# The q, k and v projections of a hybrid attention layer as one Strassen level

## The chip, the core and the metric

The kernel runs on one core of a Trainium2 chip. The metric is the device time of one execution in microseconds, the median of three runs. The profile shows one execution in which a hardware profiler recorded every instruction. The engines are TensorE (PE in the profile, PEld for its weight loads), VectorE (DVE), ScalarE (ACT), GpSimd (POOL) and SyncE (SP), which here issues nearly all transfers. Each engine takes its own instructions in the order in which the program lists them.

## The reference

One layer over 1024 tokens of width 1024, all in fp32:

```python
xn = rms_norm(x, norm_g)
proj = xn @ w_in                                  # [1024,1024] x [1024,4096]
qa, ka, va, za, qb, kb, vb, zb = split(proj)      # 512 columns each
qa, ka, qb, kb = rms_norm of each over groups of 64 columns
oa = diff_attention(qa, ka, va)                   # dense, two softmaxes a head
ya = rms_norm(oa) * silu(za)
yb = neighbourhood_attention(qb, kb, vb) * silu(zb)
x  = x + concat(ya, yb) @ w_out
x  = x + sigmoid(x @ w_ple_gate) * (p @ w_ple_proj)
```

The change concerns the six blocks kb, vb, qb, ka, va and qa of proj. The two gate blocks za and zb are computed later, beside the attention.

## The kernel before

Every large product is made of three matmuls: the operands are split into a high part in a reduced fp32 format and a low part that holds what is left, and high x high, high x low and low x high are added up in PSUM. A matmul takes 128 rows of depth, 128 tokens and 512 columns ("128x512").

The program first computes p @ w_ple_proj (lines with pps) and normalises x tile by tile. A tile is 128 tokens: `x_norm` (L228) gives xhat, `x_trans` (L240) or `x_trans_all` (L252) transposes it on TensorE, and ScalarE and VectorE take the high and the low part out of PSUM (xh, xl). Then the six blocks follow in the order kb, vb, qb, ka, va, qa, each over eight token tiles. `inproj` (L268) issues 8 x 3 matmuls for one block and tile, at L273, L274 and L275. The weights of a block come in four chunks: `load_w` (L147) loads 256 x 512 values (512 KB), 24 times in all; `split_w` (L152) multiplies them by the norm gain ng while it splits them, on ScalarE (L160) and VectorE (L161).

The result of two tiles stands in one PSUM buffer (ips). For a query or key block `qk_norm1` (L283) squares and sums it and takes the power -1/2 on GpSimd (L291, a 128x16 operand), `qk_norm2` (L294) scales it into qn, `qk_trans` (L299) transposes it (eight transposes, qtp), splits it, and the parts are stored in DRAM. For a value block `v_evac` (L344) copies or splits and stores it. The scaling and the transposes of two tiles come one and two tiles later in the order. Those of the last two tiles of qa stand inside the loop of neighbourhood attention (its rounds 1, 2 and 3, stores in round 4).

The order of every engine is that of the code, written out by hand. Transfers stand in SP's queue in that order too. While ScalarE, VectorE and GpSimd work on one tile, TensorE goes on with the next block's matmuls. GpSimd's part in the projection is the low part of half of the p weights (L172), the powers of the norms (L236 for x, L291), and the issue of a few casting transfers for the attention's constants. Neighbourhood attention begins with its scores (nsp, L534), VectorE's maximum and ScalarE's exponential (nas, L549 and L554), scaling (L562) and transposes (ntp, L572); dense attention follows, with the output projection and the gate behind it.

## Time and profile before

| | |
|---|---|
| median of three runs | 839.13 us (838.38 to 840.76) |
| the profiled execution: its span | 836.4 us |
| TensorE busy | 810.0 us, 97% |
| VectorE, ScalarE, GpSimd busy | 429.2, 395.6, 221.5 us |
| the matmuls of the six blocks | L273 to L275, 1152 of them |

The page gives no other time for the profiled execution than its span; the median of the timed runs lies 2.7 us above it. A busy time is the union of an engine's instructions; the mean duration of one matmul counts the overlap with its neighbour, so the pace of matmuls is read from starts. "Idle before, releaser" names what ended a wait.

### The profile page before, as it was taken

How to read it: one execution, taken by the hardware profiler on the slowest of the kernel's cores; microseconds unless marked ns; L12 is line 12 of the kernel's file. 1: busy time of each engine (PE TensorE's matmuls, PEld its weight loads, DVE VectorE, ACT ScalarE, POOL GpSimd, SP SyncE). 2: the span in 40 equal slices, each digit the busy share in tenths (PEclk: the TensorE clock that was granted, in tenths of full speed). 3: DMA queues.
4: the chain of work that ended last, by engine and by line, in shares of the span. 5: the costliest groups of instructions: out<-in, count | busy, mean ns of one | idle time of the engine just before them, and what ended most of it. 6: DMA issues, size and time to landing. Idle time of an engine off the chain costs nothing.

```text
span 836.4 us, 12140 instructions
## 1 busy us (share of the span) xinstructions
PE 810.0 (97%) x4386; PEld 673.8 (81%) x4386; DVE 429.2 (51%) x934; ACT 395.6 (47%) x776; POOL 221.5 (26%) x239
## 2 busy tenths in 40 slices
PE   8999999999999999699998999999999999999997
PEld 7788888888888887577876777888888878888885
DVE  4546521454432245356664678777777752732332
ACT  6435321233221214365655578889888861411120
POOL 1013100332211221011111124676767761200000
PEclk9999999999999999989999999999999999999999
DMA  8635333355353976657676778768685536323222
GB/s 295 217 126 199 111 122 124 76 128 148 113 191 131 251 177 193 177 144 194 161 201 198 180 238 217 210 149 222 171 236 157 160 107 247 124 76 101 86 91 88
DMA packets 110683, 136.72 MB, mean 163 GB/s; under 512 B 22904, under 2 KB 73752, under 8 KB 110624
## 3 DMA queue, kind: packets, MB, share of 16 engines
q1 hardware_dynamic: 108832, 130.19, 54.4%
q0 software_dynamic: 1792, 5.77, 2.3%
q8 instruction: 35, 0.57, 0.3%
q14 instruction: 24, 0.20, 0.1%
HBM read 93.95 MB, written 41.98 MB: 163 GB/s over the span
## 4 chain that ended last, share of the span: by engine, by line
PE 83%; DMA 6%; ACT 3%; DVE 3%; SPq 3%; issue 1%; POOL 1%; DVEq 0%; ACTq 0%; POOLq 0%
PE ips L273 10%; PE ips L275 10%; PE ips L274 10%; PE dsp L865 7%; PE gps L1060 3%; PE gps L1058 3%; PE gps L1059 3%; PE dtp L907 3%; PE ntp L572 2%; PE zps L469 2%; PE zps L471 2%; PE zps L470 2%; SPq L93 2%; PE pps L205 2%; PE npv L587 2%; PE dpv L934 2%
## 5 line engine op out<-in xcount | busy, mean ns | idle before, releaser
L273 PE MATMUL ips<-wh,xh 128*128 128x512 f32 x384 | 151.7, 395 | 0.0
L275 PE MATMUL ips<-wh,xl 128*128 128x512 f32 x384 | 149.8, 390 | 0.0
L274 PE MATMUL ips<-wl,xh 128*128 128x512 f32 x384 | 149.6, 389 | 0.0
L291 POOL TENSOR_TENSOR qrs<-qms,nhalf 128x16 f32<-128x16 f32 x16 | 50.3, 3143 | 186.0 <-DVE qms L289 175.0
L890 POOL TENSOR_TENSOR s<-s,s 128x1024 f32<-128x1024 f32 x32 | 77.2, 2412 | 58.1 <-ACT s L889 43.6
L275 PEld LDWEIGHTS ips<-wh,xl 128*128 128x128 f32 x384 | 72.1, 188 | 15.2
L273 PEld LDWEIGHTS ips<-wh,xh 128*128 128x128 f32 x384 | 72.1, 188 | 14.6 <-issue 0.3
L274 PEld LDWEIGHTS ips<-wl,xh 128*128 128x128 f32 x384 | 72.2, 188 | 14.3
L875 DVE CUSTOM_DVE_ANT_0 s<-dsp,T 128x1024 f32<-128x1024 f32 x64 | 77.7, 1215 | 0.0
L877 ACT ACTIVATE s<-s,dm 128x1024 f32<-128x1024 f32 x64 | 73.3, 1145 | 3.6 <-DVE dm L875 3.6
L865 PE MATMUL dsp<-K,Q 128*128 128x512 f32 x256 | 69.4, 393 | 1.4 <-DVE dm L875 1.4
L914 DVE TENSOR_TENSOR aTl<-dtp,aTh 128x512 fp32r<-128x512 f32 x64 | 44.2, 691 | 48.6 <-ACT aTh L908 48.6
L469 PE MATMUL zps<-xh,zw 128*128 128x512 f32 x128 | 54.7, 427 | 0.0
L865 PEld LDWEIGHTS dsp<-K,Q 128*128 128x128 f32 x256 | 46.1, 189 | 10.5 <-issue 1.3
L603 POOL TENSOR_TENSOR yb<-nay,yb 128x128 fp32r<-128x128 f32 x32 | 15.8, 493 | 146.1 <-ACT yb L602 146.1
L574 ACT ACTIVATE PT<-ntp 96x768 f32<-96x768 f32 (+1 forms) x32 | 25.9, 811 | 56.0 <-PE ntp L572 56.0
L471 PE MATMUL zps<-xh,zw 128*128 128x512 f32 x128 | 51.4, 402 | 0.0
L470 PE MATMUL zps<-xl,zw 128*128 128x512 f32 x128 | 51.3, 400 | 0.0
L1058 PE MATMUL gps<-wgh,x1h 128*128 128x512 f32 x128 | 50.4, 394 | 0.0
L1060 PE MATMUL gps<-wgh,x1l 128*128 128x512 f32 x128 | 49.8, 389 | 0.0
L1059 PE MATMUL gps<-wgl,x1h 128*128 128x512 f32 x128 | 49.8, 389 | 0.0
L908 ACT ACTIVATE aTh<-dtp 128x512 fp32r<-128x512 f32 x64 | 38.0, 594 | 24.7 <-PE dtp L907 24.5
(156 smaller groups left out, 1664.8 us busy)
## 6 DMA issues: line engine op xcount, KB each, us to landing
wraw<-in_w_in_dram SPq DMA_DIRECT2D x24, 512.0 KB
x<-in_x_dram SPq DMA_DIRECT2D x8, 512.0 KB
ppd<-pp SPq DMA_DIRECT2D x8, 512.0 KB
zraw<-in_w_in_dram SPq DMA_DIRECT2D x8, 512.0 KB
K<-kbh SPq DMA_DIRECT2D x8, 512.0 KB
Q<-qbh SPq DMA_DIRECT2D x16, 256.0 KB
Q<-qah SPq DMA_DIRECT2D x16, 256.0 KB
Q<-qal SPq DMA_DIRECT2D x16, 256.0 KB
```

Source lines behind the costliest of these rows:

```text
L273: mm(ps, xh(kc, a, b), wh[:, o], start=(kc == 0), stop=False)
L274: mm(ps, xh(kc, a, b), wl[:, o], start=False, stop=False)
L275: mm(ps, xl(kc, a, b), wh[:, o], start=False, stop=(kc == 7))
L469: mm(ps, w[:, 0, kc], xh(kc, a, b), start=(kc == 0), stop=False)
L471: mm(ps, w[:, 1, kc], xh(kc, a, b), start=False, stop=(kc == 7))
L865: mm(ps[:, cs], q[g][:, m, u * P:(u + 1) * P], k[:, cs], start=(g == 0), stop=(g == 1))
L875: V.tensor_tensor_reduce(out=s, in0=ps, in1=back(Td[h][:, :], 1919 - (896 - P * qt), [[-1, S]]), scale=-1.0, scalar=BIG, op0=OP.add, op1=O ...
L877: act(s, s, AF.Exp, bias=mx, scale=-1.0, accum_out=z[:, m:m + 1])
L890: G.tensor_tensor(s1, s1, s2, op=OP.add)
L1058: mm(ps, h[:, k], wh, start=(k == 0), stop=False)
L1059: mm(ps, h[:, k], wl, start=False, stop=False)
L1060: mm(ps, l[:, k], wh, start=False, stop=(k == 7))
```

## The change

The six blocks are now computed in pairs: (kb, vb), (qb, ka), (va, qa). For a pair the normed x is cut into four quarters (A11 and A12: tokens 0 to 511, first and second half of the depth; A21 and A22: tokens 512 to 1023), and the pair's weights into four quarters (rows by halves, columns by block). One level of Strassen's method in Winograd's form gives the four quarters of the result from seven products instead of eight, P1 to P7. The left operands are A11, A12, A22 and the sums S1 = A21 + A22, S2 = S1 - A11, S3 = A11 - A21, S4 = A12 - S2; the right ones are quarters of the weights and sums of them. Each product is a step for two token tiles and one for the other two: 4 x 2 x 3 = 24 matmuls a step, 42 steps.

The sums of weights run on GpSimd (`w_sum`). Weights now come as 128 x 512 chunks (256 KB), one per term of a sum and 136 in all; in the first two pairs P7's sum is kept from P6 and used in P4. The norm gain is no longer multiplied into the weights but into xhat, from a copy of the gain that is broadcast to all partitions (ngb, 512 KB). S1 to S4 are made when tiles 4 to 7 are transposed (`x_trans`), through one scratch buffer stmp, A21 is stored in DRAM and loaded again before neighbourhood attention, where the gate blocks need it. The products are added up partly in PSUM and partly in SBUF by `step_evac` (U2, U3 and the finished block C). All of qa is normalised, transposed and stored before neighbourhood attention begins. Two pools of buffers are merged, and the gate weights are split four chunks at a time.

```diff
-    def inproj(c, t, ps, k0=0, k1=8):
-        a, b = t * P, t * P + P
-        for kc in range(k0, k1):
...
-            mm(ps, xh(kc, a, b), wh[:, o], start=(kc == 0), stop=False)
-            mm(ps, xh(kc, a, b), wl[:, o], start=False, stop=False)
-            mm(ps, xl(kc, a, b), wh[:, o], start=False, stop=(kc == 7))
+    ORDER = (("P1", "P2", "P6", "P7", "P4", "P5", "P3"),) * 2 + (("P1", "P2", "P6", "P5", "P3", "P7", "P4"),)
+    LEFT = dict(P1="A11", P2="A12", P6="S2", P5="S1", P3="S4", P7="S3", P4="A22")
+    def w_sum(j):
...
+        if pi in SHARED and pr_ == "P6":
+            (_, r), (_, o), (_, q) = ts
+            G.tensor_tensor(r, r, o, op=OP.subtract)
+            t3[pi, k] = r
+            G.tensor_tensor(q, q, r, op=OP.add)
...
+        for sg, o in ts[1:]:
+            G.tensor_tensor(r, r, o, op=OP.add if sg > 0 else OP.subtract)
+    def w_split(j):
...
+        act(w[:, 0], r, AF.Copy)
+        V.tensor_tensor(w[:, 1], r, w.bitcast(F32)[:, 0], op=OP.subtract)
+    def step_mm(i, k0, k1):
...
+        for k in range(k0, k1):
+            w = wts[pi, pr_, k]
+            for u in range(2):
...
+                mm(ps, lh[:, k, a:a + P], w[:, 0], start=(new and k == 0), stop=False, skip_group_check=cont)
+                mm(ps, lh[:, k, a:a + P], w[:, 1], start=False, stop=False, skip_group_check=cont)
+                mm(ps, ll[:, k, a:a + P], w[:, 0], start=False, stop=(k == 3), skip_group_check=cont)
+    def step_evac(i):
...
+        if pr_ == "P1":
+            act(U[0][:, hs], ps, AF.Copy)
+        if pr_ == "P6":
+            V.tensor_tensor(U[0][:, hs], ps, U[0][:, hs], op=OP.add)
+        if pr_ == ORDER[pi][3]:
+            V.tensor_tensor(U[1][:, hs], ps, U[0][:, hs], op=OP.add)
+        c = TA([P, 2, 512], n="C")
+        if pr_ == "P2":
+            act(c, ps, AF.Copy)
+        else:
+            V.tensor_tensor(c, ps, U[pr_ == ORDER[pi][5]][:, hs], op=OP.add)
-        V.tensor_scalar(hat, xt, rs, None, op0=OP.mult)
+        V.scalar_tensor_tensor(hat, xt, rs, ngb, op0=OP.mult, op1=OP.mult)
+    def x_trans(t):
...
+        a21, s1, s2, s4 = [XA["tmp"][:, j] for j in range(4)]
+        act(a21, pt[0], AF.Copy)
+        sp = TA([P, 2, 4, P], F32R, n="a21s")
+        act(sp[:, 0], pt[0], AF.Copy)
+        V.tensor_tensor(s1, pt[1], a21, op=OP.add)
+        split("A22", ts, pt[1], V)
+        G.tensor_tensor(s2, s1, f("A11", 0), op=OP.subtract)
+        G.tensor_tensor(s2, s2, f("A11", 1), op=OP.subtract)
+        split("S2", ts, s2, V)
+        split("S1", ts, s1, V)
+        G.tensor_tensor(s4, f("A12", 0), s2, op=OP.subtract)
+        G.tensor_tensor(s4, s4, f("A12", 1), op=OP.add)
+        split("S4", ts, s4, V)
+        V.tensor_tensor(sp[:, 1], a21, sp.bitcast(F32)[:, 0], op=OP.subtract)
+        pst.append(lambda: st(a21d[:, :, :, ts], sp))
+        G.tensor_tensor(a21, f("A11", 0), a21, op=OP.subtract)
+        G.tensor_tensor(a21, a21, f("A11", 1), op=OP.add)
+        split("S3", ts, a21, V)
+    for i in range(len(steps) + 2):
+        w_load(6 + 2 * i)
+        step_mm(i, 0, 2)
+        got = step_evac(i - 1) if 0 < i <= len(steps) else None
+        w_split(4 + 2 * i)
+        for n, t0, c, rs in ready:
+            qk_norm2(c, rs)
...
+        w_load(7 + 2 * i)
+        if i in hooks:
+            hooks[i]()
+        step_mm(i, 2, 3)
...
+        for n, t0, c, rs in ready:
+            qk_trans(n, t0, c)
+        w_split(5 + 2 * i)
+        w_sum(6 + 2 * i)
+        w_sum(7 + 2 * i)
+        step_mm(i, 3, 4)
+        ple_st()
```

(`split` copies to the high part on ScalarE and takes the low part on VectorE; the hooks of rounds 2, 3 and 4 transpose tile 4, tile 5, and tiles 6 and 7.)

How the change moves instructions is shown at three places. The first is GpSimd's queue in the first block, before the change; xrs are the norms of x tiles, qrs those of query and key blocks.

```order
L236 TENSOR_TENSOR xrs_281<-xms_279,nhalf_83 128x1
L236 TENSOR_TENSOR xrs_379<-xms_377,nhalf_83 128x1
L236 TENSOR_TENSOR xrs_458<-xms_456,nhalf_83 128x1
L291 TENSOR_TENSOR qrs_511<-qms_509,nhalf_83 128x16
L236 TENSOR_TENSOR xrs_546<-xms_544,nhalf_83 128x1
L236 TENSOR_TENSOR xrs_629<-xms_627,nhalf_83 128x1
L291 TENSOR_TENSOR qrs_698<-qms_696,nhalf_83 128x16
L236 TENSOR_TENSOR xrs_728<-xms_726,nhalf_83 128x1
```

After the change the same stretch of GpSimd's queue holds the sums for tiles 4 and 5 (stmp), with weight sums (wraw) and the first key block's norm between them.

```order
L375 TENSOR_TENSOR stmp_626<-stmp_626,xh_165 128x512
L376 TENSOR_TENSOR stmp_626<-stmp_626,xl_166 128x512
L379 TENSOR_TENSOR stmp_626<-xh_167,stmp_626 128x512
L380 TENSOR_TENSOR stmp_626<-stmp_626,xl_168 128x512
L384 TENSOR_TENSOR stmp_626<-xh_165,stmp_626 128x512
L385 TENSOR_TENSOR stmp_626<-stmp_626,xl_166 128x512
L196 TENSOR_TENSOR wraw_530<-wraw_530,wraw_532 128x512
L198 TENSOR_TENSOR wraw_534<-wraw_534,wraw_530 128x512
L196 TENSOR_TENSOR wraw_552<-wraw_552,wraw_554 128x512
L198 TENSOR_TENSOR wraw_556<-wraw_556,wraw_552 128x512
L409 TENSOR_TENSOR qrs_696<-qms_694,nhalf_83 128x16
L375 TENSOR_TENSOR stmp_626<-stmp_626,xh_165 128x512
```

What were single small powers is now six sums a tile, and the sums for tile 5 stand behind four weight sums and the power qrs_696. Two more tiles of six sums follow, with one power ahead of the first of them.

The second place is TensorE's queue in the first block, tile 2, before the change: matmuls on xh and xl with transposes of x (xtp) and products of p (pps) between them.

```order
L273 MATMUL ips_349<-wh_270,xh_103 128x512
L274 MATMUL ips_349<-wl_271,xh_103 128x512
L275 MATMUL ips_349<-wh_270,xl_104 128x512
L273 MATMUL ips_349<-wh_270,xh_103 128x512
L274 MATMUL ips_349<-wl_271,xh_103 128x512
L275 MATMUL ips_349<-wh_270,xl_104 128x512
L246 MATMUL xtp_487<-idn_81,xhat_375 128x128 x2
L246 MATMUL xtp_492<-idn_81,xhat_375 128x128 x2
L205 MATMUL pps_497<-wph_87,ph_449 128x512 x2
```

After the change this is TensorE's queue in step 4, the first with the left operand S2 (xh_610, xl_611): three matmuls on tile 5, later ones on tile 4 again; the transposes of tiles 6 and 7 (xtp) and, a little on, those of the first key block (qtp) stand among its matmuls.

```order
L229 MATMUL ips_745<-w_654,xh_610 128x512
L230 MATMUL ips_745<-w_654,xh_610 128x512
L231 MATMUL ips_745<-w_654,xl_611 128x512
L361 MATMUL xtp_775<-idn_81,xhat_559 128x128 x4
L361 MATMUL xtp_776<-idn_81,xhat_559 128x128 x4
L361 MATMUL xtp_806<-idn_81,xhat_584 128x128 x4
L361 MATMUL xtp_807<-idn_81,xhat_584 128x128 x4
L229 MATMUL ips_745<-w_684,xh_610 128x512
L230 MATMUL ips_745<-w_684,xh_610 128x512
L231 MATMUL ips_745<-w_684,xl_611 128x512
L229 MATMUL ips_745<-w_684,xh_610 128x512
```

The transposes of tiles 6 and 7 have moved behind matmuls that read the sums of tiles 4 and 5.

The third place is GpSimd's queue at the end of the projection, before the change: norms, and the casting transfers of the attention's key constants.

```order
L291 TENSOR_TENSOR qrs_1724<-qms_1722,nhalf_83 128x16
L291 TENSOR_TENSOR qrs_1807<-qms_1805,nhalf_83 128x16
L291 TENSOR_TENSOR qrs_1892<-qms_1890,nhalf_83 128x16
L615 DMA K_364_2195<-in_pen_dram 64x1024 x2
L615 DMA K_365_2198<-in_pen_dram 64x1024 x2
L620 DMA Q_366_2201<-in_onehot_dram 64x512 x2
```

After the change the same queue around the last product of the third pair, P4, has three sums for each of its four weight chunks between the norms of the last query blocks.

```order
L409 TENSOR_TENSOR qrs_2597<-qms_2595,nhalf_83 128x16
L203 TENSOR_TENSOR wraw_2563<-wraw_2563,wraw_2565 128x512
L203 TENSOR_TENSOR wraw_2563<-wraw_2563,wraw_2567 128x512
L203 TENSOR_TENSOR wraw_2563<-wraw_2563,wraw_2569 128x512
L203 TENSOR_TENSOR wraw_2599<-wraw_2599,wraw_2601 128x512
L203 TENSOR_TENSOR wraw_2599<-wraw_2599,wraw_2603 128x512
L203 TENSOR_TENSOR wraw_2599<-wraw_2599,wraw_2605 128x512
L409 TENSOR_TENSOR qrs_2668<-qms_2666,nhalf_83 128x16
L203 TENSOR_TENSOR wraw_2632<-wraw_2632,wraw_2634 128x512
L203 TENSOR_TENSOR wraw_2632<-wraw_2632,wraw_2636 128x512
L203 TENSOR_TENSOR wraw_2632<-wraw_2632,wraw_2638 128x512
L203 TENSOR_TENSOR wraw_2670<-wraw_2670,wraw_2672 128x512
```

The norms qrs_2668 and qrs_2745 (the row behind these) have moved behind six sums each.

## Rows read from the trace of the kernel before

**Rows 1.** Page part 1: busy time, share of the span, instructions.

```profile
span 836.4 us, 12140 instructions
PE 810.0 (97%) x4386; PEld 673.8 (81%) x4386; DVE 429.2 (51%) x934; ACT 395.6 (47%) x776; POOL 221.5 (26%) x239
```

**Rows 2.** Page part 2: TensorE and its granted clock, 40 slices in tenths.

```profile
PE   8999999999999999699998999999999999999997
PEclk9999999999999999989999999999999999999999
```

**Rows 3.** Stretches: us, busy us (x instructions) by engine, granted clock, DMA share, GB/s.

```profile
0.00:25.00 25.00, 22.65 (x98) 18.43 (x99) 13.35 (x29) 17.49 (x35) 4.62 (x10) 1.00 0.82 281
...
100.00:200.00 100.00, 100.00 (x461) 82.76 (x460) 35.57 (x59) 26.39 (x48) 16.39 (x5) 1.00 0.45 119
```

**Rows 4.** Chain of waits, 150 to 185 us: start us, us, what.

```profile
...
155.99 0.87 PE qtp L306 x8
...
167.77 0.87 PE qtp L306 x8
...
179.55 0.87 PE qtp L306 x8
```

**Rows 5.** Timeline, TensorE, 12 to 24 us: start, us, line, tiles, xcount [idle before].

```profile
12.21 0.38 PE L188 MATMUL tp<-idn,p 128*128 128x128 f32 x2
...
22.71 0.47 PE L273 MATMUL ips<-wh,xh 128*128 128x512 f32 x1
```

**Rows 6.** Groups by line: busy us, mean ns of one | idle before.

```profile
L291 POOL TENSOR_TENSOR qrs<-qms,nhalf 128x16 f32<-128x16 f32 x16 | 50.3, 3143 | 186.0 <-DVE qms L289 175.0 <-DVE sclw L797 11.0
L914 DVE TENSOR_TENSOR aTl<-dtp,aTh 128x512 fp32r<-128x512 f32 x64 | 44.2, 691 | 48.6 <-ACT aTh L908 48.6
...
L908 ACT ACTIVATE aTh<-dtp 128x512 fp32r<-128x512 f32 x64 | 38.0, 594 | 24.7 <-PE dtp L907 24.5
L296 DVE TENSOR_TENSOR qn<-ips,qrs 128x1024 f32<-128x1024 f32 x16 | 19.6, 1223 | 30.6 <-POOL qrs L291 30.6
L287 DVE TENSOR_REDUCE qss<-sq 128x16 f32<-128x1024 f32 x16 | 19.5, 1219 | 18.1 <-ACT sq L285 17.1
L285 ACT ACTIVATE sq<-ips 128x1024 f32<-128x1024 f32 x16 | 16.6, 1037 | 17.2 <-PE ips L275 17.2
L319 DVE SCALAR_TENSOR_TENSOR stl<-qtp,gk,sth 128x512 fp32r<-128x512 f32 x16 | 11.3, 746 | 24.5 <-ACT sth L318 24.5
```

**Rows 7.** Source lines L172 and L838: ns min/median/max, first and last start.

```profile
L172 POOL TENSOR_TENSOR wpl<-wpr,wph x2: 1278/1284/1289, 9.0 to 10.3; 128x512 fp32r<-128x512 f32 x2
...
L838 POOL TENSOR_TENSOR oev<-oev,xr x16: 1270/1299/2307, 523.0 to 695.5; 128x512 f32<-128x512 f32 x16
```

**Rows 8.** Timeline, VectorE and GpSimd around 160 and 685 us.

```profile
159.97 1.41 DVE L161 SCALAR_TENSOR_TENSOR wl<-wraw,ng,wh 128x512 fp32r<-128x512 f32 x2
160.21 3.27 POOL L291 TENSOR_TENSOR qrs<-qms,nhalf 128x16 f32<-128x16 f32 x1 [9.13 <-DVE qms L289]
...
685.50 1.27 DVE L640 SCALAR_TENSOR_TENSOR wol<-wor,sclw,woh 128x1024 fp32r<-128x1024 f32 x1
685.61 2.31 POOL L838 TENSOR_TENSOR oev<-oev,xr 128x512 f32<-128x512 f32 x1
```

**Rows 9.** Timeline, TensorE and VectorE, first scores of neighbourhood attention.

```profile
347.88 0.88 PE L587 MATMUL npv<-PT,Vw 96*64 96x128 f32 x12
357.19 1.54 PE L572 MATMUL ntp<-idn,nas 128*128 128x128 f32 x6 [8.43 <-DVE nas L562]
...
354.28 0.56 DVE L549 CUSTOM_DVE_ANT_1 nas<-nsp,R 128x384 f32<-128x384 f32 x1 [10.95 <-DMA qah<-sth]
```

**Rows 10.** Stretches behind that idle: columns as in rows 3.

```profile
352.00:354.00 2.00, 0.00 (x0) 0.00 (x0) 0.00 (x0) 0.00 (x0) 0.00 (x0) 0.67 1.01 314
354.00:362.00 8.00, 4.81 (x16) 4.23 (x17) 3.45 (x13) 4.18 (x12) 0.46 (x1) 0.50 0.45 137
362.00:364.00 2.00, 2.00 (x10) 1.35 (x10) 1.97 (x6) 1.11 (x4) 0.46 (x1) 0.77 1.03 226
```

More of the change, by code (lines that the diff above doesn't have):

```diff
@@ L105, in layer_kernel @@
     G = nc.gpsimd
[L108 to L114 removed]
+    pt_ = T8([P, 8, 256], n="p")
     wpr = T8([P, 2, D], n="wpr")
@@ L144, in layer_kernel @@
+    chunks = [(pi, pr_, k) for pi in range(3) for pr_ in ORDER[pi] for k in range(4)]
+    steps = [(pi, pr_, h) for pi in range(3) for pr_ in ORDER[pi] for h in range(2)]
     raws = {}
     wts = {}
[L147 to L162 removed]
+    t3 = {}
@@ new lines, in layer_kernel, with w_load @@
+    SHARED = (0, 1)
+    def w_load(j):
+        if j >= len(chunks):
+            return
+        pi, pr_, k = chunks[j]
+        terms = RIGHT[pr_]
+        if pi in SHARED:
+            terms = {"P7": (), "P4": ((1, 1, 0), (-1, 0, 0))}.get(pr_, terms)
+        ts = []
+        for sg, rh, ch in terms:
+            r = T2([P, 512], n="wraw")
+            c, r0 = COL[PAIRS[pi][ch]], rh * 512 + k * P
+            ld(r, w_in[r0:r0 + P, c:c + 512])
+            ts.append((sg, r))
+        raws[j] = ts
@@ new lines, in w_sum @@
+    def w_sum(j):
+        if j >= len(chunks):
+            return
+        pi, pr_, k = chunks[j]
+        ts = raws[j]
+        if pi in SHARED and pr_ == "P7":
+            raws[j] = t3[pi, k]
+            return
+        if pi in SHARED and pr_ == "P4":
+            ts.insert(1, (-1, t3.pop((pi, k))))
+        if pi in SHARED and pr_ == "P6":
[3 more added lines that the diff above has]
+            G.tensor_tensor(q, q, r, op=OP.add)
+            raws[j] = q
+            return
+        r = ts[0][1]
+        for sg, o in ts[1:]:
+            G.tensor_tensor(r, r, o, op=OP.add if sg > 0 else OP.subtract)
+        raws[j] = r
@@ new lines, in w_split @@
+    def w_split(j):
+        if j >= len(chunks):
+            return
+        r = raws.pop(j)
+        w = T4([P, 2, 512], F32R, n="w")
+        wts[chunks[j]] = w
+        act(w[:, 0], r, AF.Copy)
+        V.tensor_tensor(w[:, 1], r, w.bitcast(F32)[:, 0], op=OP.subtract)
+    psb = {}
+    def step_mm(i, k0, k1):
+        pi, pr_, h = steps[i]
+        new = pr_ in ("P1", "P6", ORDER[pi][3], ORDER[pi][5])
+        if new and k0 == 0:
+            psb[h] = PS2([P, 2, 512], "ips")
+        cont = not new
+        lh, ll = XA[LEFT[pr_]]
+        for k in range(k0, k1):
+            w = wts[pi, pr_, k]
+            for u in range(2):
+                a = (2 * h + u) * P
+                ps = psb[h][:, u]
+                mm(ps, lh[:, k, a:a + P], w[:, 0], start=(new and k == 0), stop=False, skip_group_check=cont)
+                mm(ps, lh[:, k, a:a + P], w[:, 1], start=False, stop=False, skip_group_check=cont)
+                mm(ps, ll[:, k, a:a + P], w[:, 0], start=False, stop=(k == 3), skip_group_check=cont)
@@ L621, in na_consts, with load_r0 @@
             Q2.append(q)
+    def load_r0():
+        t = T8([P, 2, 752], n="R0")
+        Rt[0] = [t[:, h] for h in range(2)]
+        for h in range(2):
+            ld(t[:, h], ap_of(rpbp, h * 23 * 48 + 1, [[48, 8], [1, 16], [1, 752]]))
     sclw = CT([P, 2], n="sclw")
@@ new lines, in layer_kernel @@
+    w_load(0)
+    w_load(1)
+    load_p(1)
+    w_load(2)
+    w_load(3)
+    load_x(1)
+    load_p(2)
+    load_p(3)
+    load_x(2)
+    warm(4)
+    ple_t(0)
+    warm(4)
+    split_ple(0)
+    ple_t(1)
+    split_ple(1)
+    x_tiles("A11", "A12", "A22")
+    for j in range(4):
+        w_sum(j)
+    x_norm(0)
+    ple_mm(0)
+    ple_t(2)
+    w_split(0)
+    x_norm(1)
+    ple_mm(1)
+    ple_t(3)
+    w_split(1)
+    x_trans(0)
+    ple_mm(2)
+    ple_st()
+    w_split(2)
+    x_trans(1)
+    x_norm(2)
@@ new lines, in layer_kernel, with s0, s1 @@
+    ple_mm(3)
+    ple_st()
+    w_split(3)
+    for j in range(4, 6):
+        w_load(j)
+        w_sum(j)
+    load_x(3)
+    x_norm(3)
+    for i in range(2):
+        V.tensor_scalar(gk[:, i:i + 1], gv[:, 2 * i:2 * i + 1], gv[:, 2 * i + 1:2 * i + 2], 0.125,
+                        op0=OP.mult, op1=OP.mult)
+    def s0():
+        ple_t(4)
+        x_trans(2)
+        ple_mm(4)
+        x_norm(4)
+        x_trans(3)
+    def s1():
+        ple_t(5)
+        ple_mm(5)
+        x_norm(5)
+        ple_t(6)
+        ple_t(7)
```

344 lines of the change are left out of this document (145 added, 199 removed).

## The prediction

> **What bounds the kernel now.** I read the busy times first. TensorE works 810.0 of 836.4 us, VectorE 429.2, ScalarE 395.6 and GpSimd 221.5 [rows 1]; the granted clock of TensorE stands at full (2.4 GHz) in all but one of the 40 slices [rows 2]. Then I cut the stage that changes out of the span: from 100 to 200 us TensorE is busy in every microsecond, while GpSimd works 16.39 of them, in 5 instructions, and VectorE 35.57 [rows 3]. So the projection is bound by TensorE, and a matmul less is time saved, as long as nobody else becomes late. The chain of waits gives the pace: the groups of eight transposes start 11.78 us apart with 48 matmuls between them, and take 0.87 [rows 4], so one 128x512 matmul costs (11.78 - 0.87)/48 = 0.227 us. (Its row as a group says 391 ns; neighbours overlap.) The reader should see that GpSimd's 16% in this stage is that of an engine with a few jobs that stand alone; the change hands it a chain.
>
> **The parts of the change.** The sum is made on the profiled execution, span 836.4 us; the median of the three timed runs, 839.13, lies 2.7 above it, and I add these 2.7 at the end.
>
> *Matmuls removed.* 6 blocks x 8 tiles x 24 = 1152 become 42 steps x 24 = 1008. 144 x 0.227 = **-32.7 us**, the whole possible gain. It is sure as busy time.
>
> *Start.* Before, the first transposes of p beyond tile 1 come at 12.21 us and the first projection matmul at 22.71 [rows 5]. Now p of tiles 2 and 3 is loaded behind a second tile of x, the broadcast gain and two weight chunks: 3.5 MB up to its end where before about 2 MB stood ahead of everything needed by then. 1.5 MB at 281 GB/s, the rate of the first 25 us [rows 3], is 5.3 us; about 1 of it may be slack. I take **+4.5**, ends 0 and +6.
>
> *The chain of sums of quarters of x.* This decides. In tiles 4 to 7 the left operands S2, S4 and S3 are made by six GpSimd instructions a tile, and all four tiles share one scratch buffer (stmp), so that a tile starts only when the one before has left it. Durations: a GpSimd 128x512 sum of two inputs 1.28 us [rows 7]; GpSimd's power on 128x16 3.27 [rows 8], on the mean 3.14; ScalarE 128x512 0.59; VectorE 128x512 0.69; ScalarE 128x1024 1.04; VectorE 128x1024 (reduce or scale) 1.22 [rows 6]. Let time run from the end of tile 4's transposes. ScalarE copies A21 (0.59), VectorE makes S1 (0.69), GpSimd S2 (2 x 1.28): done at about 4.0. S4 follows, 6.5. S3 overwrites A21 and so waits for ScalarE's copy of S4 (0.59) and behind it, in VectorE's order, for the low parts of S4 and A21 (2 x 0.69): start 8.5, end 11.1. Then GpSimd's order has four weight sums (5.1, to 16.2) and the power of a key block; that one's input waits for ScalarE's copy of the block (1.04), a weight split and two squares, which in ScalarE's order stand behind S3's copy: it is ready at 16.5, and the power ends at 19.8. Only then S2 of tile 5: 22.4. By the same steps: S3 of tile 5 ends at 29.6, ScalarE has 3.4 us of block copy, splits and squares before it may copy A21 of tile 6, the second power ends at 38.1, S2 of tile 6 at 40.7, S3 of it at 47.8, S2 of tile 7 at 53, S3 of it at 60.1. Behind its low part (61.4) VectorE still has two lows of transposes, two weight lows, the sum of step 4 and the scaling of the second key block (5.3 in all), which TensorE's transposes in step 5 wait for: 66.7. These and the last six matmuls (0.87 + 1.36) end at 68.9.
>
> Without a wait TensorE would need 84 matmuls (19.1) and five groups of eight transposes (4.4) to that point, 23.4. It takes its queue in order and nothing else of the projection can pass, so it stands still for 68.9 - 23.4 = **+45.5 us**: some 14 before the second tile of step 4, 5 to 10 before the first block's transposes, the rest in step 5. Bounds: had GpSimd never to wait, its 20 sums to S2 of tile 7, four weight sums and two powers would end at 1.3 + 25.6 + 5.1 + 6.5 = 38.5, the operand be split at 39.8, against 17.1 when step 5 could start: at least +22. At most +54 (next part).
>
> *GpSimd beside VectorE.* Where VectorE runs an instruction with two inputs in SBUF, the trace shows GpSimd's sum waiting: 2.31 us at 685.61 beside VectorE's of 685.50, against 1.27 to 1.30 for most of its 16 [rows 7, 8]. The low parts that the change adds are of this kind. But the scaled weight low at 159.97, also with two such inputs, leaves the power at 160.21 at 3.27, near the mean of 3.14 [rows 6, 8]. In the chain S4 meets the lows of S2 and S1 (1.38) in each of four tiles, and two or four weight sums meet a weight low (0.69). I take **+3**, near the middle; ends 0 and +8.
> The Trainium skill has a rule for this (SBUF — State Buffer, "Who interferes with whom"): a VectorE instruction with two SBUF inputs and a GpSimd one that reads SBUF contend for an exclusive lock, and the one issued later waits for the whole of the other. By that rule every one of those meetings costs, the end at +8; the row at 685.61 agrees, the pair at 159.97 does not, or only because a power reads too little to show it.
>
> *Clock.* After the one long idle of before, 8.43 us to 357.19 [rows 9], the granted clock is at half (1.2 GHz) from 354 to 362, with 4.81 us of matmuls in it [rows 10]: 2.4 us lost. The stalls above are as long; what follows the first ones is hidden by the chain itself, what follows the last is not: **+2.5** (0 to +4).
>
> *Pairs two and three.* A step with a query or key block gives VectorE two weight lows (1.38), the sum with the partial sum (1.22), reduces (1.22), scaling (1.22) and lows of transposes (1.49) [rows 6], 6.5 us, against 24 x 0.227 + 0.87 = 6.3 on TensorE; ten such steps follow one another in two runs: +2. In the last product of pair three the weights need three sums a chunk: 12 x 1.28 and two powers stand in GpSimd's queue, 21.9 us, for two steps of 6.3 and one of slack, and 16 loads of 256 KB, 4.2 MB, come in the same two steps, 15 us at 281 GB/s: a stall of 3 to 8, and clock behind it: +8. Together **+10** (0 to +20).
>
> *Start of neighbourhood attention.* VectorE's first score waited for a query store and its reload (10.95 us), and TensorE's 8.43 us came of it [rows 9]. The last query pair is now normalised and stored before, so these 8.4 and the 2.4 of slow clock go. Late next is VectorE's queue: a block sum, a value low and the gate's weight low (3 x 1.22) ahead of the same scores and scaling (354.28 to 357.19, about 3): 6.7, and 2 of clock. On GpSimd's queue the constants of these queries now stand behind the four powers of pair three and are issued in the last step; TensorE's last 24 matmuls cover them, or they are part of the upper end. Net **-2** (-8 to +4).
>
> *Covered.* The copies to the weights' high parts on ScalarE (84 for 48) and the gain multiplied into x on VectorE lie beside matmuls in a stage where these engines work about a third: nothing, unless they stand in the chain, where they are counted above.
>
> Sum: 836.4 - 32.7 + 4.5 + 45.5 + 3 + 2.5 + 10 - 2 = 867.2, with the 2.7 outside the span **870 us**.
>
> **Rivals.**
> (A) *The sums hide, the saving shows.* If GpSimd's chain ended before each step that needs it: 839.1 - 32.7 = 806. For it: GpSimd's 16% in the stage. Against: step 5 wants S2 of tile 7 at 17.1, and GpSimd's bare work ends at 38.5.
> (B) *GpSimd packed.* The engines that feed it keep ahead, and TensorE waits only the +22; start +2, later stages 0, attention -2: 839.1 - 32.7 + 22 = 828 with a spread of 822 to 842. This is faster than before; it decides when the stall stays below about 30. Against: the scratch buffer and the in-order copies on ScalarE and VectorE, which I counted instruction by instruction.
> (C) *GpSimd waits at every such meeting*, its sums 2.31 us there: +8 for +3, 875, in my own range. For it the sum at 685.61, against it the power at 160.21 [rows 8]. (It is what the rule of the Trainium skill's page SBUF — State Buffer, named above, would make of this kernel.)
> (D) *Transfers bind in pair three.* Its 56 loads of 256 KB are 14.7 MB, and about as much again is stored or loaded for what follows (an estimate from the tile sizes): 30 MB at 281 GB/s is 107 us for 14 steps of 6.3 = 88, +19: 889, up to 900. SP issues all of it in order, now with the store of A21 in pair one and its reload of 2 MB before, and a store whose data is late holds the loads behind it. Against: peaks above 300 GB/s are seen for short stretches [rows 10].
>
> **How the numbers follow.** The forecast 0.58, (C) 0.11, (D) 0.12, (B) 0.14, of which 0.05 within 0.3%, (A) 0.05. Three runs of before differ by 2.4 us, 0.3%, so less than that can't be told from no change. Faster by more: 0.05 + 0.09 = 0.14; same 0.05; slower 0.81. With all low ends together the sum is 820, with all high ends 894; half of the way down and two thirds of the way up, 845 to 886, is the forecast's own range. The range reaches down to the top of (B) and up to the start of (D): 838 to 890.
>
> **What would show it.** Right: in the first pair TensorE's idle before the second product of S2 and before the transposes of the key block, released by VectorE's lows, over 40 us in all; GpSimd busy with L375 to L385 in one broken row; the granted clock at half behind these gaps; no 8 us gap at the first scores of attention, or a shorter one. Wrong: GpSimd's sums much shorter than 1.28 us, TensorE full through pair one, or the larger part of the idle in pair three with SP's queue as the releaser.

## The result, and the profile after

The changed kernel takes 917.79 us (median of 4 runs, 915.91 to 918.31), the kernel before 839.94 in the runs beside it (838.38 to 842.98): 1.092 of its time, 95% interval 1.0895 to 1.0945. It is slower, as forecast, but by 78 us instead of 31: 27.8 above the upper end of the range. The profiled execution has a span of 916.4 us, 80.0 longer than that of before.

Page parts 1 and 2 of the changed kernel: busy time by engine, then TensorE and its granted clock in 40 slices of 22.9 us, in tenths.

```profile
PE 808.3 (88%) x4242; PEld 658.1 (72%) x4242; DVE 522.8 (57%) x972; ACT 424.1 (46%) x792; POOL 351.2 (38%) x331
...
PE   7893449999899977469989799999999999999997
...
PEclk9996669999999988769999899999999999999999
```

Against [rows 1, 2] TensorE has fewer matmuls and the same busy time, and two holes, at 69 to 137 us and around 340 to 400, with the granted clock lowered in and behind both. GpSimd works 351.2 us for 221.5. No engine but TensorE is above 57%: a busy share doesn't show who is late here.

Four landmarks cut the 80.0 us into stages:

| stage | before, us | after, us | difference | forecast |
|---|---|---|---|---|
| start, to the first projection matmul (ips) | 22.7 | 26.4 | +3.7 | +4.5 |
| projection, to the first score matmul (nsp) | 294.5 | 348.3 | +53.8 | +28.3 |
| neighbourhood attention, to the first dsp | 163.9 | 182.7 | +18.8 | -2 |
| the rest | 355.3 | 359.0 | +3.7 | 0 |

The timeline of TensorE in the changed kernel, the rows that begin behind an idle time (in brackets, with what ended it):

```profile
34.25 0.95 PE L305 MATMUL pps<-wph,ph 128*128 128x512 f32 x2 [3.79 <-ACT ph L291]
...
75.91 0.80 PE L229 MATMUL ips<-w,xh 128*128 128x512 f32 x1 [4.96 <-ACT C L255]
...
86.57 0.80 PE L229 MATMUL ips<-w,xh 128*128 128x512 f32 x1 [9.01 <-ACT xh L350]
...
119.07 0.79 PE L229 MATMUL ips<-w,xh 128*128 128x512 f32 x1 [11.21 <-ACT xh L350]
...
132.47 1.94 PE L422 MATMUL qtp<-idn,C 128*128 128x128 f32 x8 [7.51 <-DVE C L413]
...
342.10 1.97 PE L422 MATMUL qtp<-idn,C 128*128 128x128 f32 x8 [6.05 <-DVE C L413]
...
357.07 1.97 PE L422 MATMUL qtp<-idn,C 128*128 128x128 f32 x8 [6.83 <-DVE C L413]
...
398.02 0.79 PE L548 MATMUL zps<-xh,zw 128*128 128x512 f32 x1 [20.08 <-DVE zw L524]
```

The reader should see three places: the chain of pair one (75 to 133), the end of pair three (342 and 357), and the longest one, 20.08 us at the start of attention, where the forecast had expected the 8.43 of [rows 9] to go. Three groups of the same eight transposes cost 1.94 to 1.97 us for 0.87 [rows 4]: the granted clock is at its lower level behind these waits. The same kernel's stretches (columns as in [rows 3]) show what the waits do to TensorE and its clock:

```profile
75.00:100.00 25.00, 10.80 (x38) 7.66 (x38) 15.55 (x20) 10.47 (x18) 16.10 (x11) 0.65 0.07 21
100.00:125.00 25.00, 11.54 (x28) 7.28 (x28) 11.23 (x13) 6.47 (x11) 17.23 (x13) 0.53 0.08 26
125.00:150.00 25.00, 17.53 (x71) 14.45 (x72) 14.75 (x17) 7.87 (x13) 15.23 (x11) 0.86 0.85 281
...
375.00:400.00 25.00, 3.33 (x11) 2.32 (x11) 5.44 (x14) 2.20 (x5) 0.00 (x0) 0.59 0.78 231
```

From 75 to 125 us no engine is busy for more than 17.23 of 25 us; each waits for another. At 375 to 400 GpSimd does nothing, VectorE little, and the DMA engines are busy 0.78: that stretch waits for transfers.

The chain of waits of the changed kernel through pair one (start us, us, what; about one piece in nine is shown):

```profile
62.61 0.61 DVE stmp L372
...
64.66 1.31 POOL stmp L376
...
67.41 1.63 POOL stmp L380
...
69.73 0.69 DVE xl L351
...
73.72 1.27 POOL wraw L196
...
77.36 1.53 DVE w L213
...
80.37 2.92 POOL qrs L409
...
84.60 1.27 POOL stmp L376
...
99.59 2.92 POOL qrs L409
...
103.84 1.28 POOL stmp L376
...
117.09 1.27 POOL stmp L376
...
131.19 1.15 DVE C L413
```

This is the chain that the prediction counted, in its order: S2 of a tile, S4, the low parts, the weight sums, the power of a key block, S2 of the next tile. TensorE's transposes of tile 4 end at 61.69. Counted from there, S2 of tiles 4, 5, 6, 7 (each the end of L376) is done at 4.3, 24.2, 43.4 and 56.7 us, forecast 4.0, 22.4, 40.7 and 53; the second key block is scaled at 70.7, forecast 66.7; step 6 starts at 75.1 (136.77), where 23.4 without a wait makes the stall 51.7, forecast 45.5 + 3 + 2.5 = 51.

At the start of attention SyncE's queue (issues of the changed kernel: start us, us that the queue spends on them) reads

```profile
369.03 11.18 SPq L97 DMA_DIRECT2D Vw<-vb  x6
380.31 1.26 SPq L97 DMA_DIRECT2D Q<-qbh  x2
...
384.79 0.97 SPq L97 DMA_DIRECT2D zraw<-in_w_in_dram  x1
386.14 3.84 SPq L100 DMA_DIRECT2D vah<-vah  x1
...
390.59 0.82 SPq L100 DMA_DIRECT2D qah<-sth  x1
```

and VectorE's timeline there

```profile
394.79 0.46 DVE L626 CUSTOM_DVE_ANT_1 nas<-nsp,R 128x288 f32<-128x288 f32 x1 [11.75 <-DMA vah<-vah]
```

The buffer that VectorE needs for its first score still holds a value block, whose store is issued only at 386.14, behind loads that fill the queue from 369.03 on. VectorE sits 11.75 us; the weights zw stand behind it in its order, and TensorE waits for them. The last row sets a sentence of the section on the change right: the last query pair is transposed before the first score matmul (372.45 against 374.71), but its store is issued only at 390.59, behind the same loads.

### The profile page after: what moved, and what is told of

It reads as the page before. It is cut to its first block, busy times and chain, and to the rows that moved or that the text cites. A ratio compares the mean times of both kernels' runs of the same rounds, so it can differ in the third digit from the quotient of the medians.

```text
span 916.4 us, 12354 instructions
## 1 busy us (share of the span) xinstructions
PE 808.3 (88%) x4242; PEld 658.1 (72%) x4242; DVE 522.8 (57%) x972; ACT 424.1 (46%) x792; POOL 351.2 (38%) x331
## 4 chain that ended last, share of the span: by engine, by line
PE 62%; DMA 13%; POOL 7%; DVE 6%; ACT 4%; SPq 3%; issue 3%; DVEq 0%; POOLq 0%; ACTq 0%
DMA wraw<-in_w_in_dram 6%; PE dsp L1006 6%; PE ips L229 4%; PE ips L230 4%; PE ips L231 4%; PE gps L1199 3%; PE gps L1200 3%; PE gps L1201 3%; PE zps L548 3%; PE dtp L1048 3%; PE ntp L649 3%; PE zps L546 3%; PE zps L547 3%; PE pps L305 2%; DMA uad<-zth 2%
## 5 line engine op out<-in xcount | busy, mean ns | idle before, releaser
L229 PE MATMUL ips<-w,xh 128*128 128x512 f32 x336 | 139.7, 416 | 28.5 <-ACT xh L350 20.8
L230 PE MATMUL ips<-w,xh 128*128 128x512 f32 x336 | 136.8, 407 | 1.2 <-DVE w L213 1.2
L231 PE MATMUL ips<-w,xl 128*128 128x512 f32 x336 | 136.8, 407 | 0.1
L213 DVE TENSOR_TENSOR w<-wraw,w 128x512 fp32r<-128x512 f32 x84 | 73.6, 881 | 59.7 <-ACT w L212 58.7
L229 PEld LDWEIGHTS ips<-w,xh 128*128 128x128 f32 x336 | 65.7, 196 | 46.5 <-ACT xh L350 22.7
L203 POOL TENSOR_TENSOR wraw<-wraw,wraw 128x512 f32<-128x512 f32 x52 | 76.8, 1490 | 46.7 <-DMA wraw<-in_w_in_dram 44.6
L212 ACT ACTIVATE w<-wraw 128x512 fp32r<-128x512 f32 x84 | 51.8, 630 | 90.4 <-POOL wraw L203 70.5
L231 PEld LDWEIGHTS ips<-w,xl 128*128 128x128 f32 x336 | 65.3, 194 | 17.9 <-DVE xl L351 2.2
L230 PEld LDWEIGHTS ips<-w,xh 128*128 128x128 f32 x336 | 65.7, 195 | 16.5 <-DVE w L213 2.1
L409 POOL TENSOR_TENSOR qrs<-qms,nhalf 128x16 f32<-128x16 f32 x16 | 48.0, 3001 | 44.5 <-DVE qms L407 44.5
```

The source lines that it names most:

```text
L203: G.tensor_tensor(r, r, o, op=OP.add if sg > 0 else OP.subtract)
L213: V.tensor_tensor(w[:, 1], r, w.bitcast(F32)[:, 0], op=OP.subtract)
L229: mm(ps, lh[:, k, a:a + P], w[:, 0], start=(new and k == 0), stop=False, skip_group_check=cont)
L230: mm(ps, lh[:, k, a:a + P], w[:, 1], start=False, stop=False, skip_group_check=cont)
L231: mm(ps, ll[:, k, a:a + P], w[:, 0], start=False, stop=(k == 3), skip_group_check=cont)
```

## The experiments

Each edit is to the changed kernel unless its diff names another. The gain is the median against the 917.79 us of the changed kernel; the ratio, with its 95% interval, is against runs of the kernel before on the same chip. Beside the experiments the kernel before took 838.85 to 840.70 us, so a gain of 2 us or less says nothing.

**The chain of pair one: half of the sums.** The three second sums are left out, and with them the low parts of A11 and A12 in the operands S2, S4 and S3.

```
-        G.tensor_tensor(s2, s2, f("A11", 1), op=OP.subtract)
-        G.tensor_tensor(s4, s4, f("A12", 1), op=OP.add)
-        G.tensor_tensor(a21, a21, f("A11", 1), op=OP.add)
```

> Edit: of the six GpSimd sums for tiles 4 to 7 the three that take in the low parts of A11 and A12 are left out (the left operands S2, S4 and S3 then lack these low parts). Theory 1 (the GpSimd chain sets the idle of pair one): three sums of 1.27 us fewer in a tile, one of them already ahead of S2, so some 11 of them go from the path to S2 of tile 7 and S3 of it: 14 us less than the changed kernel, 904 (900 to 908), nearly all before step 6. Rival (ScalarE's and VectorE's in-order copies, or the transfers, set it, GpSimd only follows): at most 4 us less, 914 or more.

899.83 us, 1.0737 (1.07 to 1.0774), a gain of 18.0, just beyond the range expected (900 to 908). Step 6 starts at 120.39 instead of 136.77: 16.4 of it in pair one. The timeline of GpSimd in this run has the sum of S2 at

```profile
63.31 1.29 POOL L375 TENSOR_TENSOR stmp<-stmp,xh 128x512 f32<-128x512 f32 x1 [2.60 <-DVE stmp L372]
...
79.29 1.25 POOL L375 TENSOR_TENSOR stmp<-stmp,xh 128x512 f32<-128x512 f32 x1
...
94.51 1.27 POOL L375 TENSOR_TENSOR stmp<-stmp,xh 128x512 f32<-128x512 f32 x1
```

15 to 16 us apart, where the chain above has 19 to 20 (83.29 less 63.28, 102.51 less 83.29). The three sums of 1.3 us that a tile lost are on the path whole: the chain sets the stall, not the transfers.

**The same sums on VectorE.** Six lines change their engine:

```
-        G.tensor_tensor(s2, s1, f("A11", 0), op=OP.subtract)
+        V.tensor_tensor(s2, s1, f("A11", 0), op=OP.subtract)
 ...
```

> Edit: the six sums of quarters run on VectorE (0.69 us each) instead of GpSimd. Theory 1: weight sums and powers no longer stand between the tiles, a tile's round becomes about 11.4 us of VectorE and its waits for ScalarE plus 2 to 3 of VectorE's other work: S2 of tile 7 some 13 us earlier than the 56.7 us of the changed kernel, time 905 (897 to 910). Rival (only the queue of GpSimd's other work matters): VectorE's in-order queue becomes as long, no gain, 915 to 922.

905.0 us, 1.0778 (1.0736 to 1.0821), a gain of 12.8. The time is the one expected, in part by luck: S2 of tile 7 is done 7.6 us earlier, where 13 were expected (49.1 us behind the transposes of tile 4 for 56.7), and step 6 starts 7.4 earlier, at 129.41; some 3 us more come between step 6 and attention. The low parts (L351) of the changed kernel by their inputs, as ns min/median/max:

```profile
L351 DVE TENSOR_TENSOR xl<-stmp,xh x16: 691/1140/1771, 66.7 to 126.8; 128x512 fp32r<-128x512 f32 x16
L351 DVE TENSOR_TENSOR xl<-xtp,xh x12: 678/682/693, 20.8 to 116.3; 128x512 fp32r<-128x512 f32 x12
```

and with the sums on VectorE:

```profile
L351 DVE TENSOR_TENSOR xl<-stmp,xh x16: 683/692/695, 70.0 to 119.7; 128x512 fp32r<-128x512 f32 x16
```

The same instruction with the same two SBUF inputs takes 0.69 us where no GpSimd sum runs beside it, and up to 1.77 beside one; with one input in PSUM (xtp) it never takes over 0.69. GpSimd's L380 takes 1.60 for its 1.27 in the same places. So VectorE and GpSimd do hold each other up, and VectorE pays more: the sums grow by 0.3, the lows by 0.45 at the median. This agrees with the rule of the Trainium skill (SBUF — State Buffer, "Who interferes with whom") that was weighed in the prediction; the power, with 16 columns, was not held up visibly (2.92 us in the chain).

**Finished stores ahead of the loads of attention.**

```
-        NA0 + 13: lambda: (z_split(COL["zb"], 0, 4), ...
+        NA0 + 13: lambda: (ple_st(), z_split(COL["zb"], 0, 4), ...
```

> Edit: in the last step the waiting stores of the value block are issued by SP ahead of the loads of the attention's values and queries instead of behind them. Theory (the 20.1 us idle at the first gate matmuls is VectorE's first score waiting for a buffer that a store still reads, and this store stands in SP's queue behind slow loads): the idle falls to 5 to 9 us, time 904 (900 to 908). Rival (the transfers themselves are the limit there, the DMA engines are busy 78%): no change, 915 to 919, the wait only changes its name.

913.73 us, 1.09 (1.086 to 1.0939), a gain of 4.1 where 14 were expected. The wait of 20.08 us fell to 8.29, but VectorE now has another wait later, at

```profile
428.90 0.46 DVE L626 CUSTOM_DVE_ANT_1 nas<-nsp,R 128x288 f32<-128x288 f32 x1 [5.37 <-DMA R<-in_rpb_dram]
```

for a table that stands behind the same loads. The store was the place where the delay was seen, not its source.

**Another buffer for the first scores.** The store's buffer is no longer the one that VectorE wants:

```
-        s = TA([P, 2, 384], n="nas")
+        s = T4([P, 2, 384], n="nas")
```

> Edit: the attention's scores (nas) take their buffers from the pool of 8 in which weights and queries stand, not from the pool of 6 in which the value block's parts wait for their stores. Theory (VectorE's first score waits for a buffer, not for data): the 20.1 us idle at the first gate matmuls falls to about 6, and as no store is hurried, nothing is given back: 906 (902 to 910). Rival (transfers limit there, as the gain of only 4 us with the stores ahead suggests): the idle goes, other waits for queries and values take most of it, 912 to 916.

915.92 us, 1.0869 (1.0814 to 1.0924), within the noise of the changed kernel. The wait fell from 20.08 to 7.43 us, and the attention stage became longer, 187.1 for 182.7. What was waited for changed and the time stayed, as the rival had it.

**The loads themselves two steps earlier**, with the stores first:

```
-        NA0 + 12: lambda: (na_consts_q(), load_q(0, 0), z_load(COL["zb"]), load_r0()),
+        NA0 + 10: lambda: (na_consts_q(), load_q(0, 0), z_load(COL["zb"]), load_r0()),
+        NA0 + 11: lambda: (load_v(0, 0, 0), load_v(0, 0, 1)),
```

> Edit: in the last steps of the projection the constants and the first query, bias and gate loads of the attention are issued two steps earlier, its first values two steps earlier, and the waiting stores ahead of them. Theory (the attention stage is 19 us longer than before because its loads are issued 6 to 12 us ahead of it, where the kernel before issues them 21 to 43 us ahead): the stage from the first scores to the first scores of the dense attention shrinks from 182.7 to 165 to 172 us; the buffers taken from the last weights cost pair three up to 4: 905 (900 to 910). Rival (that stage is bound by its own transfers): the stage stays above 178, or pair three loses what it gains: 912 or more.

904.64 us, 1.0775 (1.0759 to 1.0791), a gain of 13.2. Attention takes 169.7 us (373.7 to 543.4) for 182.7, and pair three pays nothing for it. SyncE's queue shows the cause in the issue of the first six loads of Vw. In this run:

```profile
355.82 8.93 SPq L97 DMA_DIRECT2D Vw<-vb  x6
```

In the kernel before:

```profile
296.65 6.08 SPq L93 DMA_DIRECT2D Vw<-vb  x6
```

They start 17.8 us ahead of the first score matmul here (373.66), 20.5 in the kernel before (317.17), and 5.7 in the changed kernel (369.03 to 374.71). The change issues attention's loads some 15 us later than before against their use, and whatever stands behind them is where the wait is seen. The stage is still some 6 us longer than in the kernel before; where these go was not told apart.

**The kernel before with its last query store ahead of the loads** (ple_st() moved to the start of its round 4):

```
+        if i == 4:
+            ple_st()
         pre(i + 1)
 ...
-        if i == 4:
-            ple_st()
```

> The kernel before, with the store of the last query pair ahead of the loads of values and gate weights of the same round in SP's queue instead of behind them (5.8 us earlier by its trace). Theory (VectorE's first scores of that round wait for a buffer that this store reads): the 8.4 us gap loses 5, and with it some of the half clock: 833 (831 to 836). Rival (given back by later loads, as in the changed kernel): 837 to 840.

839.89 us, 1.0009 (0.9994 to 1.0024): nothing, as the rival had it. The wait of 8.43 us [rows 9] is 5.06 then, and one of 4.60 stands at 449.01 where it was 1.85. So a store moved forward by itself brought nothing in the kernel before either; that the forecast's -2 was not to be had at all isn't shown by it.

**Shared sums of weights in pair three**, as pairs one and two have them:

```
-    SHARED = (0, 1)
+    SHARED = (0, 1, 2)
```

> Edit: pair three keeps the weight sum of P6 for P7 and P4 as the other pairs do: 16 loads of 256 KB and 8 GpSimd sums fewer. Theory (the two gaps of 6.1 and 6.8 us in the last product, with 5 us of half clock behind them, come from 12 sums in GpSimd's queue ahead of the powers): P4 has 8 sums, each gap loses two sums' time or more, 8 us less, 910 (905 to 913). Rival (the loads set it): the same loads of P4 are fewer too, but what is late is P5's and P3's loads ahead of it, and held buffers make it no better: 915 to 921.

909.96 us, 1.0848 (1.0815 to 1.088), a gain of 7.8. The waits of 6.05 and 6.83 us before the last transposes are 3.77 and 2.71. The waits shrink with the sums that stand in GpSimd's queue, as the prediction said; it had given them 3 to 8. But the edit takes away 16 loads as well as 8 sums. In the changed kernel GpSimd runs six sums without a wait from 334.10 to 343.17, through the first of the two stalls; ahead of the second it waits for a load:

```profile
349.08 9.07 POOL L203 TENSOR_TENSOR wraw<-wraw,wraw 128x512 f32<-128x512 f32 x6 [2.65 <-DMA wraw<-in_w_in_dram]
```

The DMA engines' share is 0.96 to 1.14 in each 10 us from 310 to 350. So sums and loads are both late there, and this run doesn't part them.

**The kernel before again**, unchanged, to see whether the pace of a matmul belongs to the kernel.

> The kernel before, unchanged. In the changed kernel a matmul of the projection costs 0.2333 us where the rows of before give 0.2273, and so in its gate stage, whose code is the same. Theory (the change has to do with it): again 0.227 us here. Rival (the chip or the day): 0.233 here too, and then 7 us of the changed kernel's projection and 3 of its tail are no effect of the change.

840.33 us in one run; its groups of eight transposes in the projection stand at 156.76, 168.54 and 180.32, 11.78 apart as in [rows 4]. In the changed kernel one projection matmul follows another by 0.2333 us (285.63 to 288.43 for twelve), not 0.227. So the slower pace belongs to the changed kernel.

**Buffers at multiples of 64 bytes.** The change drops a constant of 32 bytes a partition, and what is allocated behind it moves to odd multiples of 32. The edit pads another constant (and takes one small buffer from a pool for the room):

```
-        return sb.tile(shape, dt, name=nm(n), tag="nz", bufs=10)
+        return sb.tile(shape, dt, name=nm(n), tag="nz", bufs=9)
-    gv = CT([P, 5], n="gv")
+    gv = CT([P, 16], n="gv")
```

> Edit: one small constant of 20 bytes a partition takes 64 (and a pool of small tiles has 9 buffers for 10), so that the weights' buffers begin at a multiple of 64 bytes a partition as in the kernel before; in the changed kernel, which lost a constant of 32 bytes, they begin 32 beside it. Theory (the matmul's 0.2333 us for 0.2267 comes of the place of its operands): 0.227 in the projection again, 1008 x 0.0066 = 6.7 us and 3 in the gate stage: 908 (904 to 911). Rival (it comes of the order or of other traffic): 0.233 again, 915 to 920.

913.36 us, 1.0871 (1.084 to 1.0902), a gain of 4.4 where 10 were expected. The pace shows in the chain through the gate stage, where 48 matmuls lie between the groups of transposes x1p. Changed kernel:

```profile
839.37 0.87 PE x1p L1184 x8
851.45 0.87 PE x1p L1184 x8
```

Aligned:

```profile
836.54 0.87 PE x1p L1184 x8
848.32 0.87 PE x1p L1184 x8
```

12.08 apart for 11.78: 6 ns a matmul. In the projection a matmul is back at 0.2267 (277.77 to 280.49 for twelve). The projection is 5.6 us shorter and the rest 2.6, so the pace is what was expected, but 3.1 are given back in attention, 185.8 us for 182.7.

**The kernel before with 32 unused bytes** ahead of its buffers:

```
+    pad = CT([P, 8], n="pad")
+    nc.vector.memset(pad, 0.0)
     load_p(0)
```

> The kernel before, with 32 bytes a partition of unused constant ahead: the projection's operands stay at multiples of 64 bytes, in the gate stage the stationary operand moves to 32 beside one. Theory (the place of either operand sets the matmul's pace): 0.227 us in the projection as before, 0.233 in the gate stage, whose 384 matmuls cost 2.6 us more, and 1 to 3 in the attention: 843 (841 to 846). Rival (another cause of the slow pace): 0.227 in both, 839.

846.24 us, 1.0076 (1.006 to 1.0093): 7.0 us more than in the runs beside it (839.26), for 32 bytes that nobody reads, and more than the range expected. The same chain in this run,

```profile
767.40 0.87 PE x1p L1045 x8
779.48 0.87 PE x1p L1045 x8
791.54 0.88 PE x1p L1045 x8
```

shows the gate at 12.08 and 12.06; the projection kept 11.78, as expected. The gate's 384 matmuls carry some 2.5 of the 7.0 us; where the others go was not told apart. Why the offset costs a matmul its 6 ns stays open.

**The stores of the start behind its loads.**

```
     ple_mm(2)
-    ple_st()
 ...
     ple_mm(3)
-    ple_st()
 ...
     load_x(3)
+    ple_st()
```

> The changed kernel with the stores of the four finished rows of pp put behind the loads of x and weights of the start (SP's queue), nothing else. Theory: the store that stands 13.5 us at the head of SP's queue from 15.09 holds the weights and x of the first steps; without it TensorE's 3.79 us of idle at 34.25 and the half clock behind it go, about 6 us: 912 (909 to 914). Rival: the halves of p are late because of VectorE and ScalarE's own work, and the store is harmless: 916 or more, the idle at 34.25 stays.

911.22 us, 1.0847 (1.0824 to 1.087), a gain of 6.6. The wait of 3.79 us at 34.25 is gone; 1.14 is left, at 33.67. In the changed kernel four stores of pp stand in SyncE's queue, with the weights of the next steps behind them (first the issues, then what the queue waited for: us in all, times, longest):

```profile
15.09 13.52 SPq L100 DMA_DIRECT2D ppd<-pp  x4
...
SPq L100 <- DVE pp L309: 12.1, 3, 4.3
```

The stores are not slow: each waits for VectorE to finish its pp, and the loads behind wait with it.

**Four repairs at once**: shared sums, buffers at multiples of 64 bytes, attention's loads two steps earlier, and the one just above, all arithmetic kept.

> The changed kernel with four repairs at once, all of its arithmetic kept: shared sums of weights in pair three, buffers at multiples of 64 bytes, attention's first loads two steps earlier with the finished stores ahead, and the stores of the start behind its loads. Theory: the four losses lie in different stages and add up: 917.8 - 7.8 - 4.4 - 13.2 - 6 = 886 (882 to 890); what then remains above 840 is the chain of sums in pair one, 52 us for 33 saved, and some 25 of pairs two and three and the start. Rival: they overlap, each gives back part of what another gains (as the matmul pace did in the attention stage): 893 or more.

892.47 us, 1.0632 (1.061 to 1.0654): 25.3 of the 32.0 that the four gained apart, nearer to the rival's bound than to the theory's middle. Attention took its whole gain (168.8 us), the projection half: before the last transposes TensorE's timeline has again

```profile
334.06 1.39 PE L422 MATMUL qtp<-idn,C 128*128 128x128 f32 x8 [4.04 <-DVE C L413]
...
347.53 1.97 PE L422 MATMUL qtp<-idn,C 128*128 128x128 f32 x8 [5.28 <-DVE C L413]
```

9.3 us where shared sums alone left 6.5. The second wait is 2.6 longer, and GpSimd's timeline shows why:

```profile
338.34 2.15 POOL L699 DMA_DIRECT2D Q<-in_onehot_dram  x4
340.46 5.93 POOL L203 TENSOR_TENSOR wraw<-wraw,wraw 128x512 f32<-128x512 f32 x4
```

The casting transfers of the queries' constants, moved earlier with attention's loads, stand ahead of the last four sums in GpSimd's queue; with shared sums alone they came behind everything, at 358.82. The four losses are real but not independent.

**Pair one as plain products.** Strassen in pairs two and three alone, with the sums of x made on the way, finished stores first and shared sums in pair three:

```
-    ORDER = (("P1", "P2", "P6", "P7", "P4", "P5", "P3"),) * 2 + (...)
+    ORDER = (("a0", "b0", "a1", "b1", "c0", "d0", "c1", "d1"),
+             ("P1", "P2", "P6", "P7", "P4", "P5", "P3"), (...))
-    SHARED = (0, 1)
+    SHARED = (1, 2)
```

> Edit: the first pair is computed plainly (eight products, no sums of weights), Strassen's seven stay in pairs two and three; the sums of x are made in four stages a step apart while the first pair runs, through small scratch buffers; A21 stays on the chip and is stored once; with the stores ahead of the loads in the last step and the shared weight sums in pair three. Theory (the GpSimd chain before step 6 costs 50 us, and it is its place and not its work that costs): pair one has no wait, 48 matmuls more: 917.8 - 52 + 10.9 - 4 - 8 = 865 (857 to 875). Rival (the engines beside TensorE are short of time as a whole, wherever the sums stand): waits of the same kind in pair one or two, over 880.

882.37 us, 1.0487 (1.0447 to 1.0527), where 865 was expected: on the rival's side, though only one such wait is left in pair one, 11.82 us at 94.14. The projection is 36.3 us shorter (312.0), where some 49 were expected, and attention no shorter (184.5).

The same with aligned buffers, the start's stores behind its loads, and the norms of x tiles 6 and 7 ahead of the sums:

```
-        stage(4)
         x_norm(6)
+        stage(4)
 ...
```

> Edit: the version with a plain first pair, with three more: buffers at multiples of 64 bytes; the stores of p's products no longer ahead of weight loads in SP's queue at the start; the norms of x tiles 6 and 7 ahead of the sums of tiles 4 and 5 in GpSimd's queue. Expected from 882.4: 10 us for the pace of matmuls, 4 to 6 at the start, 6 to 10 of the 11.8 us gap at the first pair's transposes: 860 (854 to 868). Rival (VectorE beside GpSimd is the limit in pair one): that gap stays, 868 or more. By neither is it faster than the kernel before.

875.2 us, 1.042 (1.0388 to 1.0453), where 860 was expected; the wait is still 9.20 us, at 86.69, as the rival had it. VectorE's timeline in front of it:

```profile
75.74 2.30 DVE L355 SCALAR_TENSOR_TENSOR xhat<-x,xrs,ngb 128x1024 f32<-128x1024 f32 x1 [3.49 <-POOL xrs L354]
77.97 2.35 DVE L361 TENSOR_TENSOR xl<-xs,xh 128x512 fp32r<-128x512 f32 x2
...
89.49 3.47 DVE L361 TENSOR_TENSOR xl<-xs,xh 128x512 fp32r<-128x512 f32 x2
```

The norm takes 2.30 us for 1.28 elsewhere, a pair of lows 2.35 and 3.47 for 1.4: VectorE is busy 22.92 of the 25 us from 75 to 100, stretched by GpSimd's sums beside it.

And with attention's loads earlier as well (the edit shown above):

> The kernel with pair one as plain products, with attention's first loads two steps earlier as well. Theory: late loads before the attention cost about 9 beyond the late stores (13.2 with both moved, 4.1 with the stores alone, which this kernel has moved already): 875.2 - 9 = 866 (863 to 869), slower than the kernel before, since pair one still loses its 9 us stall and the half clock behind it, and pair three's steps are bound by VectorE. Rival: the loads now collide with pair three's weights, 872 or more.

865.51 us, 1.031 (1.029 to 1.033), as expected. No version ran faster than the kernel before.

## Why the prediction was right in direction and wrong in size

- **Matmuls removed, -32.7.** 144 matmuls did go. But each of the remaining ones cost 0.2333 us for 0.2267. This is a term the prediction did not have: +6.7 in the projection (1008 x 0.0066), and most of the rest's +3.7 (the aligned run's rest is 2.6 shorter). Shown by the aligned buffers and by the 32 unused bytes.
- **Start, +4.5.** Measured +3.7, and 6.5 behind it: 3.79 us of idle at 34.25, 0.47, and the half clock. The prediction counted bytes ahead of p; it did not look at the stores of pp, which wait for their data at the head of SyncE's queue. Shown by the stores behind the loads, a gain of 6.6.
- **The chain, +45.5, with +3 of contention and +2.5 of clock.** Measured 51.7 for 51: right, at each of its steps within 4 us and at the end 6.2 behind, for which it had added 5.5; shown by leaving out half the sums. Rival A (the sums hide) and rival B (GpSimd packed) fell with it; rival C's contention is there, but most of it on VectorE, where it was priced on GpSimd.
- **Pairs two and three, +10.** Measured 22: 4 in pair two, 18 at the end of pair three. The mechanism named (twelve sums and two powers in GpSimd's queue, 16 loads beside them, clock behind) was right, and its price of 8 for this end too small by 10; the two waits of 6.05 and 6.83 us carry about 5 of half clock. Shared sums gave back 7.8. How the 22 divide between GpSimd's and VectorE's queues and the loads was not told apart. Rival D's full transfers are part of it, and the 18 us lie near D's 19, so D was not refuted.
- **Start of neighbourhood attention, -2 (-8 to +4): the largest step that failed.** Measured +18.8. The prediction said of the last query pair that it "is now normalised and stored before, so these 8.4 and the 2.4 of slow clock go", and looked for what is late next in VectorE's queue. It was in SyncE's: the pair's own store is issued 16 us behind the first score, a value block's store just ahead of it, both behind six loads that take 11.18 us, and so with everything else of the stage. The loads issued two steps earlier took 13 us back; the store alone took 4, another buffer nothing.
- **Sum.** 6.7 and 3.7 of pace and rest, 5.7 of the start, 0.7 of the chain, 12 of the pairs and 20.8 of attention are 49.6; the span missed its forecast (867.2) by 49.2. So the direction came from a chain that was counted rightly, and the size was missed by four terms that lay around it. All high ends of the prediction together gave 894: attention lay 15 us above its own, and the pace was in no term.

With all four side losses repaired as far as they went, 892.47 remains; 52.9 over the 839.61 of the kernel before in the same runs. That is about the 51.7 of pair one alone, so the saving of 32.7 went into what was left of the losses in the other stages.

## What to carry to other kernels

Fewer matmuls pay only if the operands' makers keep ahead: follow one operand through the in-order queue of every engine that touches it, and add up the durations; busy shares of 17 in 25 us hid a chain without a gap. Where a change moves work across the border of a stage, ask how far ahead of it the next stage's loads are now issued (here 5.7 us for 20.5); a wait that is removed by itself (a store, a buffer) comes back at the next consumer. After a constant is added or removed, look at the pace of the untouched matmuls.
